# Starting the tiles of split weights at multiples of 128 bytes in a partition

## The chip, the cores and the metric

The kernel runs on one core of a Trainium2 chip. The metric is the device time of one execution in microseconds (us). The core's engines are named as the profile names them: PE is TensorE's matmul row, PEld its loads of the stationary operand, DVE is VectorE, ACT is ScalarE, POOL is GpSimd, and SP is SyncE, which here only issues transfers (DMAs). SBUF is the on-chip memory: 128 partitions, in each of which a tile takes a run of bytes. The start of that run, counted in bytes from the start of the partition, is the tile's address, and it is the same in every partition.

## What is computed

One layer of a decoder trunk over 256 tokens with a model width of 2048, all in float32. Almost all the work is products of activations with weights that are read once each:

```python
h = rmsnorm(x, attn_norm[l])
proj = h @ w_in[l]
...
mem_kv = rmsnorm(mem, mem_norm[l]) @ w_mem_kv[l]
...
y_gla = (o_gla * jax.nn.silu(gr)) @ w_br_gla[l]
y_sb = stick_breaking_mixer(q_sb, k_sb, sv) @ w_br_sb[l]
y_mem = memory_mixer(q_m, m_k, m_v) @ w_br_mem[l]
g = jax.nn.sigmoid(gates.reshape(B, T, N_BRANCH, D))
merged = g[:, :, 0] * y_gla + g[:, :, 1] * y_sb + g[:, :, 2] * y_mem
x = x + merged @ w_o[l]
h2 = rmsnorm(x, ffn_norm[l])
gate, up = jnp.split(h2 @ w_gate_up[l], 2, axis=-1)
x = x + (jax.nn.silu(gate) * up) @ w_down[l]
```

The three mixers between these products (gated linear attention, stick-breaking attention, attention into 256 memory tokens) are small beside them.

## The kernel before

Every weight is float32, and a product is made from three matmuls in the type fp32r. `split` (L116 to L125) turns a tile of raw weights into a high part `wh` (ACT, a cast, L121) and a low part `wl` (DVE, the difference, L122). The activations stand split in the same way, for instance as `xTh` and `xTl`. A product is then high times high, high times low, low times high: three matmuls that follow each other and add into one PSUM tile. In each of them the activations are the stationary operand (128x128, loaded by LDWEIGHTS before each matmul), and `wh` or `wl` is the moving operand, which is streamed through.

Two routines do this. `gemm` (L152) loads raw weights in tiles `raw` of 1 MB and splits them in pieces of 128x1024, each of which serves twelve matmuls of 512 columns (L176 to L178). `sgemm` (L184), used for the gates, the output projection and most of the feed-forward network, forms one step of a Strassen-like scheme on part of the depth: four quarters `rq` of 128x768 come by DMA, DVE adds them (L252), and seven products of 256 columns (L223 to L225) stand between ordinary ones of 512 columns (L246 to L248).

The tiles `wh` and `wl` come from `parts` (L148), each in a ring of `ring_bufs` buffers under its own tag. `parts` takes them from whichever of three pools is current (`kit`): `wring` for the memory and attention part (4 buffers of each), `mrg` for the merge and the output projection, and `ffn` for the feed-forward network (6 buffers of each). A tile of 128x1024 fp32r takes 4096 bytes in a partition, and the slices that matmuls read begin at whole multiples of 1024 bytes in it. In each pool other tiles lie behind the rings: `rq` in `mrg` and `ffn`, the sections and attention tiles behind `wring`, and `fh`, `fl`, `sdh`, `sdl` (the split activations of the feed-forward network) in `ffn`.

The order on each engine is the order of the code. Matmuls wait for their two operands; a cast into `wh` waits until the matmuls that read that buffer a ring earlier are done; DVE's subtraction waits for the cast. DMAs of weights are issued by SP in order, into rings of three `raw` and five `rq`. Small jobs of the mixers (`background`, taken up by `step`) are put between groups of matmuls.

Of the kernel before, what the change touches and what calls it, by code (L numbers as in the profile page):

```python
# [10 lines left out]
F32R = mybir.dt.float32r  # L11
# [5 lines left out]
P = 128  # L17
# [58 lines left out]
def trunk(ctx: ExitStack, tc: tile.TileContext, a, out):  # L76
# [6 lines left out]
    IT = 2 * NB  # L83
# [63 lines left out]

    def parts():  # L148

        return [kit.tile([P, IT], F32R, tag=f"w{x}", name=f"w{x}", bufs=ring_bufs) for x in "hl"]  # L150

    def gemm(xs, w, c0, row0=0, first=(), load=nc.sync.dma_start):  # L152

        o = [acc() for _ in range(2)]
        nk = len(xs)
        sizes = list(first)
        sizes += [min(KG, nk - k) for k in range(sum(sizes), nk, KG)]  # L160
        k0 = 0
        for n in sizes:
            xp = [x() if callable(x) else x for x in xs[k0 : k0 + n]]
            raw = loads()
            r0 = row0 + k0
            load(raw[:, :n], w[c0 // NB, :, r0 : r0 + n])
            for g in range(0, n, 2):
                m = min(2, n - g)
                wh, wl = (x[:].rearrange("p (k n) -> p k n", k=2) for x in parts())
                split(wh[:, :m], wl[:, :m], raw[:, g : g + m])  # L170
                for t in range(2):
                    s = slice(t * P, (t + 1) * P)
                    for j in range(m):
                        xh, xl = xp[g + j]
                        k = k0 + g + j
                        pe.matmul(o[t][:], xh[:, s], wh[:, j], start=k == 0, stop=False)  # L176
                        pe.matmul(o[t][:], xh[:, s], wl[:, j], start=False, stop=False)  # L177
                        pe.matmul(o[t][:], xl[:, s], wh[:, j], start=False, stop=k == nk - 1)  # L178
                step()
            k0 += n  # L180
        return o

    def sgemm(xs, forms, w, blk, row0=0, late=False):
# [22 lines left out]
        def form(src):  # L206
            hi, lo = (x[:, : SP * HB] for x in parts())
            split(hi, lo, src[:])
            return hi, lo
# [20 lines left out]
        def rest(k0, last=False):  # L230

            if k0 not in loaded:
                n = min(KG, nk - k0)
                raw = loads()
                c = ob + (k0 - 2 * SP) * NB
                nc.sync.dma_start(raw[:, :n], wb[:, c : c + n * NB].rearrange("p (k n) -> p k n", n=NB))
                for g in range(0, n, 2):
                    loaded[k0 + g] = raw[:, g : g + 2]
            wh, wl = (x[:].rearrange("p (k n) -> p k n", k=2) for x in parts())
            split(wh, wl, loaded[k0])  # L240
            for t in range(2):
                s = slice(t * P, (t + 1) * P)
                for j in range(2):
                    xh, xl = xs[k0 + j]
                    f, e = k0 + j == 2 * SP, last and j == 1
                    pe.matmul(o[t][:], xh[:, s], wh[:, j], start=f, stop=False, skip_group_check=True)  # L246
                    pe.matmul(o[t][:], xh[:, s], wl[:, j], start=False, stop=False, skip_group_check=True)  # L247
                    pe.matmul(o[t][:], xl[:, s], wh[:, j], start=False, stop=e, skip_group_check=True)  # L248
            step()
# [187 lines left out]
    kit = wring = tc.alloc_tile_pool(name="wring", bufs=1)  # L437
    ring_bufs = 4
# [406 lines left out]
    kit = mrg = tc.alloc_tile_pool(name="mrg", bufs=1)  # L845
    ring_bufs = 6
# [27 lines left out]
    hl = xpool.tile([P, KD, T], F32R, name="hl", tag="xTl")  # L874
# [25 lines left out]
    kit = ctx.enter_context(tc.tile_pool(name="ffn", bufs=1))  # L900
# [4 lines left out]
    for part in (range(0, 4), range(4, 8), range(8, NF)):  # L905
        fs, tiles = [], []
        for j in part:
# [6 lines left out]
            f = [kit.tile([P, 4, T], F32R, name=f"f{x}", bufs=4) for x in "hl"]  # L914
# [78 lines left out]
```

## Time and profile before

| | us |
|---|---|
| median of 3 runs | 1693.62 (1692.26 to 1694.8) |
| the profiled execution | 1692.7 |
| its span, first to last instruction | 1690.9 |
| PEld busy in the span | 1427.2 (84%) |
| DVE busy | 1286.2 (76%) |
| ACT busy | 930.7 (55%) |

The profiled execution is 0.92 us below the median, and 1.8 us of it lie outside its span. In the rows of the profile, "wh<-raw 128x1024" is an instruction that writes `wh` and reads `raw`; "acc<-wh,hl" is a matmul into the PSUM tile `acc` with `wh` as the moving operand and `hl` as the stationary one. The duration of a matmul includes its way through the array, so that matmuls overlap each other; what one costs is read from the distance between two starts. The column PEclk is the granted share of TensorE's clock.

### The profile page before, as it was taken

Reading aid. Unit: us, or ns where it says so; the run is one execution under the profiler, and the core shown is the slowest. Engines: PE = TensorE matmul, PEld = TensorE weight load, DVE = VectorE, ACT = ScalarE, POOL = GpSimd, SP = SyncE. Lnnn points to the kernel's source line nnn. Section 1 sums busy time; section 2 is a strip of 40 time slices with the busy share of each in tenths; the row PEclk is TensorE's granted clock in tenths of the full one; section 3 lists DMA queues with packets and bytes.
Section 4 is the critical chain, followed back from the end, with each engine's and each line's share of the span. In section 5 each row is a group of like instructions: output and inputs, shape, how many; then the busy total and the mean of one; then the engine's idle time right before and its main releaser. Section 6 shows DMA issues by size and latency. Waiting matters only on the chain.

```text
span 1690.9 us, 22452 instructions
## 1 busy us (share of the span) xinstructions
PE 1673.7 (99%) x8730; PEld 1427.2 (84%) x8730; DVE 1286.2 (76%) x1585; ACT 930.7 (55%) x1231; POOL 1.3 (0%) x6
## 2 busy tenths in 40 slices
PE   8999999999999999999999999999999999999999
PEld 6888888888877888888888788888888888888887
DVE  6756566664665578877889899988889988888863
ACT  6654454664653455555556566665555565555642
POOL 0000000000000000000000000000000000000000
PEclk9999999999999999999999999999999999999999
DMA  8765445445534556564566364655564555565562
GB/s 326 265 235 188 149 152 191 156 151 198 173 129 146 199 211 213 185 233 165 184 213 202 123 225 137 236 199 199 199 200 162 196 193 186 198 206 192 178 224 100
DMA packets 68682, 322.05 MB, mean 190 GB/s; under 512 B 7504, under 2 KB 12112, under 8 KB 41440
## 3 DMA queue, kind: packets, MB, share of 16 engines
q1 hardware_dynamic: 68112, 320.17, 55.4%
q8 instruction: 68, 1.11, 0.3%
q10 hardware_dynamic: 464, 0.45, 0.1%
q14 instruction: 38, 0.31, 0.0%
HBM read 318.50 MB, written 2.10 MB: 190 GB/s over the span
## 4 chain that ended last, share of the span: by engine, by line
PE 96%; DVE 1%; DMA 1%; ACT 0%; issue 0%; SPq 0%; DVEq 0%; ACTq 0%
PE acc L176 13%; PE acc L177 13%; PE acc L178 13%; PE acc L247 11%; PE acc L248 11%; PE acc L246 11%; PE tmp L225 4%; PE tmp L224 3%; PE tmp L223 3%; PE acc L225 3%; PE acc L223 3%; PE acc L224 3%; PE tmp L336 2%; DVE wl L122 1%; DMA raw<-in_w_mem_kv 0%; PE tmp L565 0%
## 5 line engine op out<-in xcount | busy, mean ns | idle before, releaser
L122 DVE TENSOR_TENSOR wl<-raw,wh 128x1024 fp32r<-128x1024 f32 (+1 forms) x459 | 558.7, 1220 | 271.7 <-ACT wh L121 268.1
L121 ACT CAST wh<-raw 128x1024 fp32r<-128x1024 f32 (+1 forms) x459 | 480.0, 1048 | 426.6 <-PE acc L178 265.8
L121 ACT CAST wh<-rq 128x768 fp32r<-128x768 f32 x294 | 244.8, 837 | 206.5 <-PE acc L248 80.0
L122 DVE TENSOR_TENSOR wl<-rq,wh 128x768 fp32r<-128x768 f32 x294 | 278.9, 954 | 27.1 <-ACT wh L121 23.5
L176 PE MATMUL acc<-wh,xTh 128*128 128x512 f32 x576 | 230.3, 400 | 0.0
L178 PE MATMUL acc<-wh,xTl 128*128 128x512 f32 x576 | 225.0, 391 | 0.0
L177 PE MATMUL acc<-wl,xTh 128*128 128x512 f32 x576 | 224.6, 390 | 0.0
L246 PE MATMUL acc<-wh,hh 128*128 128x512 f32 x440 | 174.4, 398 | 4.2 <-ACT wh L121 4.2
L247 PE MATMUL acc<-wl,hh 128*128 128x512 f32 x440 | 174.5, 396 | 1.1 <-DVE wl L122 0.9
L248 PE MATMUL acc<-wh,hl 128*128 128x512 f32 x440 | 173.0, 393 | 0.0
L252 DVE TENSOR_TENSOR rq<-rq 128x768 f32<-128x768 f32 x168 | 160.7, 957 | 4.4
L176 PE MATMUL acc<-wh,oh 128*128 128x512 f32 x320 | 125.3, 393 | 2.9 <-ACT wh L121 2.0
L178 PEld LDWEIGHTS acc<-wh,xTl 128*128 128x128 f32 x576 | 108.1, 188 | 23.3 <-issue 0.3
L176 PEld LDWEIGHTS acc<-wh,xTh 128*128 128x128 f32 x576 | 108.3, 188 | 22.1 <-issue 1.4
L177 PEld LDWEIGHTS acc<-wl,xTh 128*128 128x128 f32 x576 | 108.4, 188 | 21.7 <-issue 0.7
L177 PE MATMUL acc<-wl,oh 128*128 128x512 f32 x320 | 125.5, 392 | 0.5 <-DVE wl L122 0.5
L178 PE MATMUL acc<-wh,ol 128*128 128x512 f32 x320 | 125.3, 392 | 0.0
L246 PEld LDWEIGHTS acc<-wh,hh 128*128 128x128 f32 x440 | 83.5, 190 | 20.0 <-ACT wh L121 4.9
L248 PEld LDWEIGHTS acc<-wh,hl 128*128 128x128 f32 x440 | 83.8, 190 | 18.1
L247 PEld LDWEIGHTS acc<-wl,hh 128*128 128x128 f32 x440 | 84.0, 191 | 16.6 <-DVE wl L122 2.2
L176 PEld LDWEIGHTS acc<-wh,oh 128*128 128x128 f32 x320 | 60.1, 188 | 17.8 <-ACT wh L121 2.5
L177 PEld LDWEIGHTS acc<-wl,oh 128*128 128x128 f32 x320 | 60.5, 189 | 13.8 <-DVE wl L122 1.1
(319 smaller groups left out, 2999.3 us busy)
## 6 DMA issues: line engine op xcount, KB each, us to landing
raw<-in_w_in SPq DMA_DIRECT2D x72, 1024.0 KB, 4.8
raw<-in_w_gate_up SPq DMA_DIRECT2D x44, 1024.0 KB, 4.9
rq<-in_w_gate_up SPq DMA_DIRECT2D x88, 384.0 KB, 4.9
raw<-in_w_down SPq DMA_DIRECT2D x28, 1024.0 KB, 4.8
raw<-in_w_gate SPq DMA_DIRECT2D x16, 1024.0 KB, 6.9
raw<-in_w_mem_kv SPq DMA_DIRECT2D x15, 1024.0 KB, 4.9
rq<-in_w_gate SPq DMA_DIRECT2D x32, 384.0 KB, 5.2
rq<-in_w_down SPq DMA_DIRECT2D x32, 384.0 KB, 4.7
```

The costliest lines, as they stand in the source:

```text
L121: act.copy(hi, src)
L122: dve.tensor_tensor(lo, src, hi.bitcast(F32), op=ALU.subtract)
L176: pe.matmul(o[t][:], xh[:, s], wh[:, j], start=k == 0, stop=False)
L177: pe.matmul(o[t][:], xh[:, s], wl[:, j], start=False, stop=False)
L178: pe.matmul(o[t][:], xl[:, s], wh[:, j], start=False, stop=k == nk - 1)
L223: pe.matmul(dst, xh, hi[:, c], start=start and i == 0, stop=False, skip_group_check=True)
L224: pe.matmul(dst, xh, lo[:, c], start=False, stop=False, skip_group_check=True)
L225: pe.matmul(dst, xl, hi[:, c], start=False, stop=stop and i == SP - 1, skip_group_check=True)
L246: pe.matmul(o[t][:], xh[:, s], wh[:, j], start=f, stop=False, skip_group_check=True)
L247: pe.matmul(o[t][:], xh[:, s], wl[:, j], start=False, stop=False, skip_group_check=True)
L248: pe.matmul(o[t][:], xl[:, s], wh[:, j], start=False, stop=e, skip_group_check=True)
L252: dve.tensor_tensor(dst[:], a[:], b[:], op=ALU.add)
```

## The change

Each tile from `parts` is asked for with a start at a multiple of 128 bytes. No argument, before, means a multiple of 32.

```diff
     def parts():
 
-        return [kit.tile([P, IT], F32R, tag=f"w{x}", name=f"w{x}", bufs=ring_bufs) for x in "hl"]
+        return [kit.tile([P, IT], F32R, tag=f"w{x}", name=f"w{x}", bufs=ring_bufs, align_bytes=128) for x in "hl"]
```

No instruction is added, removed or moved on any engine. What changes is where tiles lie. These are the addresses in the two built programs, with the remainder by 128:

| tile (pool) | before | after |
|---|---|---|
| first `wh` (`wring`) | 137824 (96) | 137856 (0) |
| first `wl` (`wring`) | 154208 (96) | 154368 (0) |
| first `wh` (`mrg`) | 119392 (96) | 119424 (0) |
| first `wl` (`mrg`) | 143968 (96) | 144128 (0) |
| first `wh` (`ffn`) | 160352 (96) | 160384 (0) |
| first `wl` (`ffn`) | 184928 (96) | 185088 (0) |
| first `rq` (`mrg`) | 168544 (96) | 168736 (32) |
| first `fh` (`ffn`) | 183904 (96) | 184096 (32) |
| `sdh` (`ffn`) | 216672 (96) | 216864 (32) |
| `raw`, all three | 20608 (0) | 20608 (0) |
| `xTh` and `hh` | 64096 (96) | 64096 (96) |

All `wh` move up by 32 bytes and all `wl` by 160; what lies behind them in a pool moves up by 192. The tiles ahead of them stay, among them the raw weights and the stationary operands `xTh`, `xTl`, `hh`, `hl`, `oh`, `ol`, and the forms `sx` and `sf`.

## The prediction

> **What bounds the kernel now.** I read the page first, then the waits, then the matmuls in order of time. The page's first, second and fourth parts:
>
> ```profile
> span 1690.9 us, 22452 instructions
> PE 1673.7 (99%) x8730; PEld 1427.2 (84%) x8730; DVE 1286.2 (76%) x1585; ACT 930.7 (55%) x1231; POOL 1.3 (0%) x6
> PE 96%; DVE 1%; DMA 1%; ACT 0%; issue 0%; SPq 0%; DVEq 0%; ACTq 0%
> ```
>
> The chain that ended last is 96% matmuls. The longest waits by engine say the same from the other side:
>
> ```profile
> ACT wh L121 <- PE acc L178: 298.4, 186, 6.5
> DVE wl L122 <- ACT wh L121: 294.6, 252, 3.4
> ACT wh L121 <- PE acc L248: 202.0, 127, 2.5
> ```
>
> ACT waits about 500 us for matmuls to free a weight buffer, and DVE waits for ACT: the makers of weights are held up by PE, not PE by them. So an edit is worth what it does to the distance between matmul starts. In a quiet stretch of `gemm` (start, duration, engine and line):
>
> ```profile
> 599.84 0.39 PE L177 MATMUL acc<-wl,oh 128*128 128x512 f32 x1
> 600.06 0.39 PE L178 MATMUL acc<-wh,ol 128*128 128x512 f32 x1
> ...
> 605.96 0.39 PE L177 MATMUL acc<-wl,oh 128*128 128x512 f32 x1
> ```
>
> From the first to the last are 27 starts, 6.12 us, so 226.7 ns for 512 columns. There are 992 matmuls of L176 and 840 of L246 (count and busy time of one line over the whole span, PE then PEld), and each is one of three lines:
>
> ```profile
> 0.00:1691.00 1691.00, 393.16 (x992) 186.46 (x992) 1.00 0.56 190
> 0.00:1691.00 1691.00, 331.71 (x840) 158.79 (x840) 1.00 0.56 190
> 0.00:1691.00 1691.00, 250.64 (x882) 168.48 (x882) 1.00 0.56 190
> ```
>
> That is (992 + 840) x 3 = 5496 long matmuls, 5496 x 226.7 ns = 1246 us or 74% of the span. The last row is L223: 882 x 3 = 2646 short ones of 256 columns. Everything below hangs on what a long one pays.
>
> **What a long matmul pays.** After a pause in which the weights came late, the clock was granted at half for 6.6 us; first the windows row (PE, PEld, DVE, ACT, POOL, then PEclk), then matmuls in it:
>
> ```profile
> 963.90:970.50 6.60, 6.50 (x14) 4.63 (x15) 6.60 (x16) 4.00 (x6) 0.00 (x0) 0.50 0.92 339
> 966.66 0.63 PE L247 MATMUL acc<-wl,hh 128*128 128x512 f32 x1
> ...
> 970.07 0.60 PE L247 MATMUL acc<-wl,hh 128*128 128x512 f32 x1
> ```
>
> Eight starts in 3.41 us are 426 ns each. With each column a cycle of the array, full clock would make that 213.1 ns. The long matmul takes 226.7 at full clock, so it loses 13.6 ns there, and none at half clock. A fixed number of array cycles, such as a swap of stationary operands, would show at both. It is rather something that cannot feed the array at full speed: 2048 bytes in each partition in 226.7 ns. The loss is one part in 16 of the stream, and 128 bytes are one part in 16 of 2048. This is why the start of the tile may matter, and why I do not write the change off. The short ones:
>
> ```profile
> 1102.03 0.28 PE L223 MATMUL tmp<-wh,hh 128*128 128x256 f32 x1
> 1102.14 0.28 PE L224 MATMUL tmp<-wl,hh 128*128 128x256 f32 x1
> ...
> 1103.10 0.60 PE L336 MATMUL tmp<-cst,cv 128*128 128x128 f32 x4
> ```
>
> The first takes about 0.11 us, the next eight 0.96 / 8 = 120 ns. Half of a long one would be 113. Loads of the stationary operand, where the matmuls have two columns only, follow each other so:
>
> ```profile
> 439.09 0.19 PEld L703 LDWEIGHTS tmp<-cr,rd 128*128 128x128 f32 x1
> ...
> 439.76 0.19 PEld L703 LDWEIGHTS tmp<-cr,rd 128*128 128x128 f32 x1
> ```
>
> Six in 0.67 us, 112 ns each. So a short matmul is paced by its load of the stationary operand rather than by its stream, and a faster stream brings it at most 120 - 112 = 8 ns.
>
> **The change part by part.** No instruction is added or moved, so there is no new wait and no new order; three things can change.
>
> *ACT and DVE on other addresses.* The trace has sources at both kinds of start: `raw` at a multiple of 128, `rq` at 96 above one (duration as min/median/max):
>
> ```profile
> L121 ACT CAST wh<-raw x459: 604/1050/1116, 4.3 to 1670.7; 128x1024 fp32r<-128x1024 f32 x152, 128x512 fp32r<-128x512 f32 x1
> L121 ACT CAST wh<-rq x294: 817/838/902, 617.3 to 1608.3; 128x768 fp32r<-128x768 f32 x147
> L121 ACT CAST sxh<-raw x2: 1477/1482/1488, 611.1 to 855.9; 128x1536 fp32r<-128x1536 f32 x2
> L122 DVE TENSOR_TENSOR wl<-raw,wh x459: 691/1225/1229, 5.1 to 1671.8; 128x1024 fp32r<-128x1024 f32 x152, 128x512 fp32r<-128x512 f32 x1
> L122 DVE TENSOR_TENSOR wl<-rq,wh x294: 947/953/961, 618.6 to 1609.1; 128x768 fp32r<-128x768 f32 x147
> L122 DVE TENSOR_TENSOR sxl<-raw,sxh x2: 1753/1756/1758, 612.7 to 857.5; 128x1536 fp32r<-128x1536 f32 x2
> ```
>
> From `raw` alone ACT takes (1482 - 1050) / 512 = 0.84 ns an element, which gives 834 ns for 768 elements; from `rq` it takes 838. DVE takes (1756 - 1225) / 512 = 1.04 ns, which gives 959; from `rq` it takes 953. So a start of 96 instead of 0 is worth -6 to +4 ns in an instruction of about 900, as far as a read goes. A write at another start is not in the trace; I give it the same bounds. 753 casts x 4 ns are 3 us of ACT, hidden under its 500 us of waiting for PE. Taken at 0. The cover is thinnest in the feed-forward part:
>
> ```profile
> 900.00:1200.00 300.00, 295.65 (x1707) 260.15 (x1707) 269.79 (x325) 178.05 (x247) 0.00 (x0) 0.99 0.56 192
> ```
>
> DVE is busy for 270 of 300 us there. Six ns more on each of its 325 instructions are 2 us, still under the 30 that it has.
>
> *Transfers into `rq` at another start* (96 before, 32 after):
>
> ```profile
> rq<-in_w_gate_up SPq DMA_DIRECT2D x88, 384.0 KB, 4.9
> raw<-in_w_gate_up SPq DMA_DIRECT2D x44, 1024.0 KB, 4.9
> ```
>
> Both kinds land in 4.9 us though one is 2.7 times as large: the start is not what sets it. DMAs are busy for 0.56 of that stretch. Taken at 0; without their cover a wait would show at the casts.
>
> *The matmul's stream.* No tile in the trace of before that a matmul streams through starts at any other remainder than 96, so the price is not in the trace. Bounds for one long matmul: below, the whole loss goes, -13.6 ns; above, the worst distance that occurs with all operands there. After each pause comes a train like this:
>
> ```profile
> 1105.29 0.39 PE L247 MATMUL acc<-wl,hh 128*128 128x512 f32 x1
> ...
> 1106.45 0.39 PE L246 MATMUL acc<-wh,hh 128*128 128x512 f32 x1
> 1106.67 0.39 PE L247 MATMUL acc<-wl,hh 128*128 128x512 f32 x1
> ```
>
> Five starts in 1.16 us, 232 ns each, before it settles at 0.22 to 0.23. So +5.3 ns is the other end. Times 5496 these ends are -75 and +29 us. I take 0, the value of the nearest rows: the loss is there in every stage alike, with ACT, DVE and DMA busy or not; it goes with the length of the stream, as the 0.11 of the first short matmul suggests; and a cost of a bad start would come once in a matmul and not in proportion to its length. [...]
>
> Sum: 0 + 0 + 0. The profiled execution of 1692.7 stays; on the median's scale (0.9 higher) that is 1693.6.
>
> **The rivals.**
>
> *The start costs the whole loss.* If the stream is fetched in pieces of 128 bytes counted from its start, each piece that starts at 96 lies across two lines of 128, and each pays one step; from 0 none does. For it: the loss is just one part in 16, which is 128 bytes' share. Against it: nothing in the trace has another start. Long matmuls fall to 213.1: 5496 x 13.6 = 75 us, 1693.6 - 75 = 1619. If short ones gain their 8 ns too, 2646 x 8 = 21 more. DVE would not stop it: 5496 in 1691 us are 975 in 300 us, 13 us saved, and 287 is still above DVE's 270.
>
> *One line fewer.* If each cross of a line of 128 costs a sixteenth of the loss, 13.6 / 16 = 0.85 ns, a stream of 2048 bytes crosses 16 such lines from 96 and 15 from 0. 5496 x 0.85 = 4.7 us: 1689.
>
> *The stream falls in with the weight loads.* The train of 232 shows that the distance depends on how the stream and the load of the next stationary operand stand to each other: same operands, same engine, another phase. Now both start at 96; after the change the stream is 32 bytes apart from the load. If that makes the phase of the train the lasting one, each long matmul costs 5.3 ns more: 1693.6 + 29 = 1723, slower. It decides as soon as the matmuls in a quiet stretch stand over 0.6 ns further apart, for 0.6 x 5496 = 3.3 us is 0.2%, about what a measurement of this kernel can tell from no change. Against it: four kinds of stationary tiles all settle at 226.7. [...]
>
> **How the numbers follow.** No change: 0.50, as all rows are met by a limit that has nothing to do with the start. The whole loss or most of it goes: 0.22, since one part in 16 fits it too well to be left out. One line fewer: 0.10. Slower by the weight loads: 0.18. So faster is 0.32, the same 0.50, slower 0.18. The predicted time is that of the likeliest, 1693.6. The range takes in the first three cases, which hold 0.82: from 1618 to 1698. The likeliest alone would be 1690 to 1697.
>
> **What would show it.** In a quiet stretch the distance of long matmuls: 226.7 for my forecast, 213 to 214 for the first rival, 225.8 for the second, 232 for the third. Short ones at 120 in all cases but the first. The casts at 838 and 1050 and the subtractions at 953 and 1225 stay within 6 ns. I am wrong if the distance moves by over 0.6 ns, or if it stays and the time does not: then the waits of ACT and DVE must show a pause that was not there.

## The result and the profile after

| | before | after |
|---|---|---|
| median, us | 1693.24 | 1717.18 (1716.49 to 1717.35, 4 runs) |
| ratio | | 1.0138 [1.0126, 1.015] |
| span of the profiled execution, us | 1690.9 | 1715.4 |

The change makes the kernel 1.4% slower. This is the third rival's result, and it lies outside the range of the prediction. One correction to the table of addresses above: in its rows for `wh`, `wl` and `rq` the labels `mrg` and `ffn` are exchanged. All their remainders are the same, so nothing of the argument hangs on it.

The page of the kernel after, its first, second and fourth parts:

```profile
span 1715.4 us, 22452 instructions
PE 1698.2 (99%) x8730; PEld 1424.8 (83%) x8730; DVE 1288.1 (75%) x1585; ACT 930.1 (54%) x1231; POOL 1.3 (0%) x6
PE 96%; DVE 2%; DMA 1%; ACT 0%; issue 0%; SPq 0%; DVEq 0%; ACTq 0%
```

PE alone has grown, by as much as the span (24.5 us). The number of instructions and the share of matmuls in the chain that ended last are what they were; DVE and ACT are busy as long as before to within 2 us. The longest waits by engine:

```profile
ACT wh L121 <- PE acc L178: 313.2, 188, 6.6
DVE wl L122 <- ACT wh L121: 312.7, 264, 3.4
ACT wh L121 <- PE acc L248: 206.0, 125, 2.0
```

ACT waits 19 us longer for PE than before, and DVE 18 us longer for ACT: the makers of weights have more time, not less. The casts and subtractions (min/median/max in ns) and the transfers (KB, median us to landing) are as they were, to within 2 ns in each median and 0.3 us in the landing:

```profile
L121 ACT CAST wh<-raw x459: 602/1050/1087, 4.2 to 1694.7; 128x1024 fp32r<-128x1024 f32 x152, 128x512 fp32r<-128x512 f32 x1
L121 ACT CAST wh<-rq x294: 817/836/863, 628.6 to 1630.9; 128x768 fp32r<-128x768 f32 x147
L122 DVE TENSOR_TENSOR wl<-raw,wh x459: 692/1224/1228, 5.0 to 1695.8; 128x1024 fp32r<-128x1024 f32 x152, 128x512 fp32r<-128x512 f32 x1
L122 DVE TENSOR_TENSOR wl<-rq,wh x294: 945/951/961, 629.9 to 1631.8; 128x768 fp32r<-128x768 f32 x147
rq<-in_w_gate_up SPq DMA_DIRECT2D x88, 384.0 KB, 4.6
raw<-in_w_gate_up SPq DMA_DIRECT2D x44, 1024.0 KB, 4.9
```

What is left is the matmul. A quiet stretch of `gemm` in order of time (start, duration, engine, line):

```profile
580.47 0.39 PE L177 MATMUL acc<-wl,oh 128*128 128x512 f32 x1
...
589.72 0.39 PE L178 MATMUL acc<-wh,xTl 128*128 128x512 f32 x1
```

From the first to the last are 40 starts in 9.25 us: 231.3 ns, where the kernel before has 226.7. The starts between these rows are 0.23, 0.23 and 0.24 us apart in turn and repeat with the three matmuls of a product. This is the quicker of two cycles that the kernel falls into: in the memory and attention part the three take 693 ns together in about a third of the products and 700 in more than half. Over all pairs of consecutive long matmuls (5254, as many as before) the sum of the distances goes from 1216.7 to 1242.6 us, +25.9; for those under 260 ns, which leaves out pauses, the mean goes from 227.9 to 232.7 ns. The sum for the short ones goes from 295.7 to 294.0, -1.7. Together that is about the growth of the span. It is spread over all stages: the kernel after is 11.1 us behind by 600 us, 17.5 by 990 and 24.5 at the last matmul.

### The profile page after: what moved, and what is told of

Same layout as the page of the kernel before. It is cut to its first block, busy times and chain, and to the rows that moved or that the text cites. A ratio compares the mean times of both kernels' runs of the same rounds, so it can differ in the third digit from the quotient of the medians.

```text
span 1715.4 us, 22452 instructions
## 1 busy us (share of the span) xinstructions
PE 1698.2 (99%) x8730; PEld 1424.8 (83%) x8730; DVE 1288.1 (75%) x1585; ACT 930.1 (54%) x1231; POOL 1.3 (0%) x6
## 4 chain that ended last, share of the span: by engine, by line
PE 96%; DVE 2%; DMA 1%; ACT 0%; issue 0%; SPq 0%; DVEq 0%; ACTq 0%
PE acc L178 14%; PE acc L177 13%; PE acc L176 13%; PE acc L248 11%; PE acc L247 11%; PE acc L246 11%; PE tmp L225 3%; PE tmp L224 3%; PE tmp L223 3%; PE acc L225 3%; PE acc L224 3%; PE acc L223 2%; PE tmp L336 2%; DVE wl L122 1%; DMA raw<-in_w_mem_kv 0%; PE tmp L537 0%
## 5 line engine op out<-in xcount | busy, mean ns | idle before, releaser
L176 PE MATMUL acc<-wh,xTh 128*128 128x512 f32 x576 | 232.5, 404 | 0.0
L178 PE MATMUL acc<-wh,xTl 128*128 128x512 f32 x576 | 227.9, 396 | 0.0
L176 PE MATMUL acc<-wh,oh 128*128 128x512 f32 x320 | 126.7, 397 | 3.0 <-ACT wh L121 2.3
L178 PEld LDWEIGHTS acc<-wh,xTl 128*128 128x128 f32 x576 | 108.1, 188 | 25.4 <-issue 0.3
L176 PEld LDWEIGHTS acc<-wh,xTh 128*128 128x128 f32 x576 | 107.9, 187 | 24.8 <-ACT wh L121 0.8
L178 PE MATMUL acc<-wh,ol 128*128 128x512 f32 x320 | 127.5, 398 | 0.0
L176 PEld LDWEIGHTS acc<-wh,oh 128*128 128x128 f32 x320 | 59.9, 188 | 19.9 <-ACT wh L121 2.7
```

## The experiments

Three theories stood at the outset. **A**: what counts is the distance between the start of the stream and the start of the stationary operand (0 before; after, 32 for `wh` and 160 for `wl`, and with `fh` and `fl`, which move up by 192 themselves, 160 and 32 the other way). **B**: a stream from a multiple of 128 is slow by itself. **C**: what counts is the distance between `wh` and `wl`, which the change makes 128 bytes larger. All edits are made to the kernel before, and all ratios are against it on the same chip.

### Everything up by 32 bytes

```diff
+    main.tile([P, 8], F32, tag="shift", name="shift", bufs=1)
```

This small tile stands ahead of all tiles but the raw weights and the constants, so `wh`, `wl` and the stationary operands all start at a multiple of 128.

> All large tiles, the stationary operands too, move up by 32 bytes, so that the weights start at a multiple of 128 as after the change, but stream and stationary operand start at the same remainder as before. Theory A (what counts is how the start of the stream stands to the start of the stationary operand that is loaded meanwhile): long matmuls at 226.7 ns, 1693 us. Theory B (a stream that starts at a multiple of 128 is slow by itself): 231 to 233 ns, 1717 us. Theory C (what counts is the distance from wh to wl, which the change made 128 bytes larger): it is as before here, so 226.7 ns, 1693 us.

Measured 1693.96 against 1694.06 us, ratio 0.9995 [0.9986, 1.0005]. Its matmuls in order of time:

```profile
568.90 0.39 PE L177 MATMUL acc<-wh,oh 128*128 128x512 f32 x1
...
578.20 0.39 PE L179 MATMUL acc<-wh,xTl 128*128 128x512 f32 x1
```

Those are 41 starts in 9.30 us, 226.8 ns each, with a stream from a multiple of 128. B falls: the new start costs nothing if the stationary operand has it too.

### Both streams up by 32, at their old distance from each other

```diff
+    PADS = {'wring': (32, 0), 'mrg': (32, 0), 'ffn': (32, 0)}
...
+            n = PADS[kit.name][i]
+            if n and (kit.name, x) not in padded:
+                padded.add((kit.name, x))
+                kit.tile([P, n // 4], F32, tag=f"pad{x}", name=f"pad{x}", bufs=1)
```

Two numbers for each pool: the bytes put ahead of `wh` and between `wh` and `wl`. What lies behind the rings moves along, so in the last stage `fh` and `fl` move with the streams. (Lines that an edit puts in raise the line numbers in the rows: L186 to L188 here are L176 to L178 before.)

> wh and wl both move up by 32 bytes, their distance stays as before; the stationary operands stay, apart from the split activations fh and fl of the feed-forward network, which lie behind the weights and move with them. Theory A: long matmuls at 230 to 235 ns, 1705 to 1730 us; only the last stage (L176 to L178 with fh and fl, the last 70 us) keeps 226.7 ns, because there both moved. Theory B: 1717 us, the last stage as slow as the others. Theory C: 226.7 ns everywhere, 1693 us.

Measured 1711.57 us, ratio 1.0101 [1.0086, 1.0116]. First the attention stage, then the last stage of the same execution:

```profile
580.83 0.39 PE L187 MATMUL acc<-wl,oh 128*128 128x512 f32 x1
...
590.16 0.39 PE L188 MATMUL acc<-wh,xTl 128*128 128x512 f32 x1
...
1675.63 0.39 PE L188 MATMUL acc<-wh,fl 128*128 128x512 f32 x1
...
1684.70 0.39 PE L186 MATMUL acc<-wh,fh 128*128 128x512 f32 x1
```

There are 40 starts in each piece: 9.33 us or 233.3 ns in the first, 9.07 us or 226.8 ns in the second. The streams start at the same remainder in both pieces; only the stationary operand has moved along in the second. C falls as the cause, for the distance of `wh` and `wl` is the old one, and A is shown with a control inside one run.

### Only `wl` moved, and other distances

Only the numbers of `PADS` change. With (0, 128) in all pools `wh` stays and `wl` goes up by 128:

> Only wl moves, by 128 bytes; wh stays. Theory A with a period of 128 bytes: 226.7 ns, 1693 us; with a longer period, matmuls of wl alone change. Theory B: the remainder by 128 is as before, 1693 us. Theory C: the distance is as after the change, 231 to 233 ns, 1717 us.

Measured 1704.67 us, ratio 1.0062 [1.0047, 1.0077]. In the memory and attention part the next start comes 231.3 ns after one of `wh`, whose distance is still 0, and 231.8 ns after one of `wl`. These means mix several cycles. In 102 of the 626 products seen whole there only `wl` is slow, as in these rows, where the starts are 0.22, 0.24 and 0.22 us apart:

```profile
574.92 0.39 PE L186 MATMUL acc<-wh,oh 128*128 128x512 f32 x1
575.14 0.40 PE L187 MATMUL acc<-wl,oh 128*128 128x512 f32 x1
575.38 0.39 PE L188 MATMUL acc<-wh,ol 128*128 128x512 f32 x1
575.60 0.39 PE L186 MATMUL acc<-wh,oh 128*128 128x512 f32 x1
```

In others all three are slow, with 236, 234 and 230 ns or 232, 232 and 234. That only matmuls of `wl` change thus holds for a part of the products. The distances of the two starts don't fix the cycle by themselves, and a matmul that is in step with its own operands can be slow beside one that isn't. Whether the distance of `wh` and `wl`, which this edit changes too, has a part in that is not shown.

Four kernels then moved both streams by amounts that differ from pool to pool:

```diff
+    PADS = {'wring': (64, 0), 'mrg': (96, 0), 'ffn': (128, 0)}
...
+    PADS = {'wring': (256, 0), 'mrg': (512, 0), 'ffn': (192, 0)}
...
+    PADS = {'wring': (384, 0), 'mrg': (160, 0), 'ffn': (320, 0)}
...
+    PADS = {'wring': (352, 0), 'mrg': (448, 0), 'ffn': (224, 0)}
```

> wh and wl move up together, by 64 bytes in the memory and attention part (the first 600 us), by 96 in the merge and output projection, by 128 in the feed-forward network. Theory A with a period of 128 bytes: 226.7 ns in the feed-forward network, other distances than 226.7 in the two parts before, to either side (213 to 240 ns). Theory B: remainders by 128 are 32, 64 and 96 and none is 0, so 226.7 ns throughout, 1693 us. Theory C: 1693 us.

> wh and wl move up together against the stationary operands: by 256 bytes in the memory and attention part, by 512 in the merge and output projection, by 192 in the feed-forward network. Theory A with a period of 256 bytes: 226.7 ns in the first two parts, about 231 in the third. With a period of 512: 226.7 in the second part alone. With no period up to 512: 226.7 nowhere but in the last stage, where fh and fl moved with the weights. If some distance is better than none, long matmuls below 226 ns show in that part.

> wh and wl move up together by 384 bytes in the memory and attention part, by 160 in the merge and output projection, by 320 in the feed-forward network. Theory A: 228 to 235 ns in all three unless the period is 128, 160 or less, 226.7 in the last stage; below 226 ns in a part where the distance is better than none. About 1705 to 1715 us.

> wh and wl move up together by 352 bytes in the memory and attention part, by 448 in the merge and output projection, by 224 in the feed-forward network. Theory A: 228 to 235 ns in all three, 226.7 in the last stage; below 226 ns in a part where the distance is better than none. About 1705 to 1715 us.

In this order they took 1707.11 us, ratio 1.007 [1.0053, 1.0087]; 1693.31, 1.0 [0.9989, 1.0012]; 1705.02, 1.0062 [1.004, 1.0085]; 1711.23, 1.0103 [1.0074, 1.0132]. The mean distance of two starts in ns, by the distance of the stream's start above that of the stationary operand (long: pairs under 260 ns, so with the trains after pauses, and over whatever cycles occur; the short ones, under 150 ns, only in `mrg` and `ffn`):

| distance, bytes | long | short |
|---|---|---|
| 0 | 227.5 to 228.6 | 119.5 |
| 32 | 233.2 | 116.8 |
| 64, and 320 | 229.3, 229.2 | 116.1 |
| 96, and 352 | 233.3, 233.4 | 119.9 |
| 128, and 384 | 232.8, 232.8 | 118.4 |
| 160 | 234.0 | 117.8 |
| 192, and 448 | 232.9, 233.1 | 114.7, 114.2 |
| 224 | 233.4 | 118.3 |
| 256 and 512 | 227.5, 227.9 | |

The pattern has a period of 256 bytes: 256 and 512 give what 0 gives, and 320, 352, 384 and 448 give what 64, 96, 128 and 192 give. The expectation of a period of 128 bytes is missed: at 128 the long matmuls take 232.8 ns. In the kernel with 256, 512 and 192, first long matmuls at a distance of 256, then short ones at 192:

```profile
569.50 0.39 PE L187 MATMUL acc<-wl,oh 128*128 128x512 f32 x1
...
578.57 0.39 PE L188 MATMUL acc<-wh,xTl 128*128 128x512 f32 x1
...
1026.03 0.28 PE L235 MATMUL tmp<-wh,sfl 128*128 128x256 f32 x1
...
1027.73 0.28 PE L235 MATMUL acc<-wh,hl 128*128 128x256 f32 x1
```

The 40 long starts take 9.07 us, 226.8 ns each. The 15 short ones take 1.70 us, 113 ns each, where the kernel before takes 120. Of the distances tried, 0 suits long matmuls best and 192 short ones; that kernel comes out even because in `ffn` the one pays for the other.

### Which stationary operand: in use, or being loaded

```diff
-    xtiles = [xpool.tile([P, KD, T], F32R, name=f"xT{x}", tag=f"xT{x}") for x in "hl"]
+    xtiles = []
+    for x in "hl":
+        xtiles.append(xpool.tile([P, KD, T], F32R, name=f"xT{x}", tag=f"xT{x}"))
+        if x == "h":
+            xpool.tile([P, 8], F32, tag="shift", name="shift")
```

All tiles behind `xTh` go up by 32, so only products with `xTh` (and `hh`, in its place) have a distance. While a matmul runs, the stationary operand of the next one is loaded (in the kernel before, the load for the matmul that starts at 600.06 starts at 599.84, together with the matmul ahead of it); if only the one in use or only the one being loaded counted, one of the three matmuls would keep its 227.

> All large tiles move up by 32 bytes, as in the run all32, but for xTh (and hh, which takes its place). So the high part of these activations starts 32 bytes below weights and low part, and everything else starts alike. Theory A: where oh, fh, sx or sf are stationary, 226.7 ns; where xTh and xTl or hh and hl are, about two in three long matmuls are slower, 228 to 235. If it is the operand loaded meanwhile that counts, the matmul of wl (during which the low part is loaded) is the one that keeps about 227, and both matmuls of wh are slow. If it is the operand in use, the matmul with the low part keeps 227, and both with the high part are slow. Theory B: about 1717 us, all slow. About 1703 us by theory A.

Measured 1706.85 us, ratio 1.0077 [1.0048, 1.0106]:

```profile
240.09 0.40 PE L176 MATMUL acc<-wh,xTh 128*128 128x512 f32 x1
...
245.45 0.39 PE L178 MATMUL acc<-wh,xTl 128*128 128x512 f32 x1
```

These are 23 starts in 5.36 us, 233 ns, and all three lines are slow (`wh,xTh` 235 to 236, `wl,xTh` 233, `wh,xTl` 231 to 232), while quiet stretches with `oh` and `fh` keep 226.7. The buffers of `wh` and `wl` that are streamed against `xTh` and against `oh` are the same, filled by ACT and DVE in the same way, so it isn't these engines' accesses that make the difference. Neither operand alone decides. The excess over 226.7 is largest (9 ns) where both operands stand apart, 6 ns where only the one in use does, and 5 ns where only the one being loaded does; that each adds a part fits this, but wasn't tested by itself, and as a matmul in step can be slow beside one out of step (the run in which only `wl` moved), the question stays open.

### What the loss is made of

The loss meant here is the prediction's estimate: 226.7 ns measured at full clock, less half of the 426 ns measured at a granted clock of 0.50, so 13.6 ns. That a long matmul can run at 213.1 ns no run shows. If the stationary operand's load takes reading time from the stream, another load should change the loss. Three kernels changed the load. The first reads every second token, with its 128 columns 8 bytes apart instead of 4 (it mixes up the order of the tokens), at distances of 128, 0 and 64 in the three pools:

```diff
-                    s = slice(t * P, (t + 1) * P)
+                    s = slice(t, t + 2 * P - 1, 2)
```

> The long matmuls read their stationary operand with a step of two tokens (one tile the even tokens, the other the odd ones, instead of the first and the second half), so the order of tokens in the output is another and the mixers work on mixed tokens; the work is the same in amount. The load of 128 columns then covers 1024 bytes instead of 512. The streams start 128 bytes above the stationary operand in the memory and attention part, at the same remainder in the merge and output projection, 64 bytes above in the feed-forward network. Theory A says that load and stream meet where they read the same lines by 256 bytes at the same time: with a load that moves on at another pace the loss of 13.6 ns itself changes, to either side, and with it the three parts differ from 226.7 and from each other. If the loss of 13.6 ns is the stream's own, long matmuls stay at 226.7 or above in all parts, none below 226.

Measured 1713.07 us, ratio 1.0108 [1.009, 1.0127]; long matmuls are 231.4, 232.8 and 233.2 ns apart. In `mrg` the starts have the distance 0 (4 bytes less for the odd tokens) and it is slow all the same, at 232.3 and 233.4 ns: equal starts didn't help a load that reads every second element. All parts lie above 226.7, so the run doesn't tell whether the loss of 13.6 ns is the load's or the stream's own. That load and stream read the same lines at the same time, as the expectation takes theory A, is not shown.

The other two load fewer columns in `gemm`, and so leave out part of the products: 64, or 16 (`P // 8` in place of `P // 2`, here with `mrg` up by 32 bytes as well).

```diff
-                        pe.matmul(o[t][:], xh[:, s], wh[:, j], start=k == 0, stop=False)
...
+                        m_ = P if k in (0, nk - 1) else P // 2
+                        s = slice(t * P, t * P + m_)
+                        pe.matmul(o[t][:m_], xh[:, s], wh[:, j], start=k == 0, stop=False)
```

> In the routine of ordinary products (L176 to L178) every matmul but those of the first and the last depth step takes 64 columns of its stationary operand instead of 128, so half of each token tile gets only two of its depth steps; the stream of 512 columns and its address stay. The load of the next operand is half as long. If the load takes the 13.6 ns from the stream: about half of it is left, 220 ns in the quiet stretches of this routine. If the stream pays it by itself: 226.7 ns as before. At 220 ns some 2500 matmuls save 6.7 ns each, 17 us.

> As half, but 16 columns of the stationary operand instead of 64 (a load of 64 bytes in a partition), and in the merge and output projection wh and wl lie 32 bytes further up. If the load reads against the stream, long matmuls of the ordinary routine fall by an eighth of the loss, to 215 to 217 ns, and in the merge part too, whatever the distance. If the stream pays by itself, 226 to 230 ns with so short a load as well; if it pays at its start by how it stands to the load's start, the merge part still differs from the memory and attention part.

They took 1699.38 us, ratio 1.0037 [1.0021, 1.0053], and 1703.27 us, 1.0061 [1.0038, 1.0084]. Loads and long matmuls with 64 columns:

```profile
574.31 0.13 PEld L180 LDWEIGHTS acc<-wh,ol 128*64 128x64 f32 x1
...
231.54 0.40 PE L178 MATMUL acc<-wh,xTh 128*64 128x512 f32 x1
...
237.99 0.39 PE L179 MATMUL acc<-wl,xTh 128*64 128x512 f32 x1
```

and with 16:

```profile
574.13 0.09 PEld L188 LDWEIGHTS acc<-wh,oh 128*16 128x16 f32 x1
...
231.32 0.40 PE L188 MATMUL acc<-wh,xTh 128*16 128x512 f32 x1
...
239.88 0.40 PE L189 MATMUL acc<-wl,xTh 128*16 128x512 f32 x1
```

The loads shrink from 0.19 to 0.13 and 0.09 us. The matmuls stand 6.45 / 28 = 230.4 and 8.56 / 37 = 231.4 ns apart: more than with full loads, though the distance is 0, and neither of the expected values (220 or 226.7 with 64 columns). A loss in proportion to the load's columns would have shrunk to a half and an eighth. With 16 columns a distance of 32 costs nothing more (230.3 ns in `mrg`, 231.1 at distance 0 in `wring`), where full loads go from 226.7 to 233: there the short load is the faster one. This fits the reading that 226.7 is a favourable cadence into which full loads from the same remainder fall, and not an undisturbed pace to which a bad start adds a cost. It isn't shown: the matmul itself also works on fewer columns here, and that wasn't tested apart from the load.

### The short matmuls alone

In the table long matmuls are best at distance 0 (227.5 to 228.6 ns) and short ones at 192 (114.7 and 114.2), and both can be had: the short ones read the first 768 of the 1024 elements of a tile, so their quarters can lie 192 bytes (48 elements) further up in it, while the long ones stay.

```diff
-            hi, lo = (x[:, : SP * HB] for x in parts())
+            hi, lo = (x[:, 48 : 48 + SP * HB] for x in parts())
```

> The kernel before, except that the split quarters (the streams of the short matmuls) lie 192 bytes further on inside their tile of 4096 bytes; long matmuls as before. Theory A, with what the runs sweep_b and sweep_d showed at a distance of 192 bytes (short ones at 113 to 114 ns instead of 120): 2646 x 6.6 ns = 17 us less, 1676 us, long ones unchanged at 226.7. If the gain of the short ones in those runs came from something else that was moved there (rq or cv), 120 ns and 1694 us.

Measured **1685.4** against 1694.25 us, ratio **0.9944 [0.993, 0.9957]**: faster than both kernels. The page, then the short matmuls of a product and what follows them:

```profile
span 1683.1 us, 22452 instructions
...
647.82 0.28 PE L224 MATMUL tmp<-wl,xTh 128*128 128x256 f32 x1
...
649.82 0.39 PE L246 MATMUL acc<-wh,xTh 128*128 128x512 f32 x1
650.05 0.39 PE L247 MATMUL acc<-wl,xTh 128*128 128x512 f32 x1
650.27 0.39 PE L248 MATMUL acc<-wh,xTl 128*128 128x512 f32 x1
650.50 0.39 PE L246 MATMUL acc<-wh,xTh 128*128 128x512 f32 x1
```

From the first row to the first long matmul are 17 starts in 2.00 us, 117.6 ns, which is also the mean; 113 came only in 17 products whose first two starts are about 0.2 us apart. The expected size is therefore missed: 2646 x 1.9 ns (119.5 less 117.6) are 5 us. Another gain was not foreseen: the long matmuls behind the short ones begin at 0.23 at once, without the train of 232, and their mean falls from 228.4 to 226.9 ns in `ffn` and from 227.9 to 226.9 in `mrg`, about 4 us together. Two more places for the quarters, the first 64 bytes up, the second 176 in `mrg` and 208 in `ffn`:

```diff
+            hi, lo = (x[:, 16 : 16 + SP * HB] for x in parts())
...
+            off = 44 if kit.name == "mrg" else 52
+            hi, lo = (x[:, off : off + SP * HB] for x in parts())
```

> As short192, but the split quarters lie 64 bytes further on inside their tile. In the run sweep_c short matmuls at this distance took 116 ns after long ones at 229. If the distance alone sets them, 116 ns here too, 2646 x 4 = 11 us less than before, 1683 us; if it is how the long matmul ahead stands in time, anything from 113 to 120, and long ones at 226.7.

> As short192, but with 176 bytes in the merge and output projection and 208 in the feed-forward network. If 192 is one point of a broad stretch, short matmuls at 113 to 115 ns in both parts; if the banks that matter are 16 or 32 bytes wide, one of the two or both at 116 to 120.

They took 1690.29 us, ratio 0.9983 [0.9972, 0.9994], and 1690.17, 0.9977 [0.9966, 0.9989], with short means of 118.0, and of 118.8 and 119.0 ns. So most of the gain is gone 16 bytes to either side of 192. That banks of 16 or 32 bytes are behind this, as the expectation supposes, no run shows. In the table short matmuls took 116.1 ns at 320 bytes, which is 64 by the period of 256, and 114.7 at 192, both times beside long ones that were out of step. So for short matmuls the distance alone doesn't set the pace; that what ran just ahead of them does too fits these runs and the products at 113, but wasn't tested by itself.

## Why the prediction was wrong

- *PE is the bound, the makers wait for it*: right. ACT's longest wait, for L178, grew from 298.4 to 313.2 us.
- *Casts and subtractions at other addresses, 0*: right. 838 became 836 ns, 1050 stayed.
- *Transfers into `rq`, 0*: right. 4.9 became 4.6 us.
- *Short matmuls, 120 ns in all cases but the first rival*: nearly. Their mean went from 119.5 to 118.7 ns, worth 1.7 us. The reason given, the pace of their loads (112 ns), was not shown: their own pace, 113 to 120 ns over the runs, moves with the distance and, as it seems, with what ran ahead of them.
- *The matmul's stream, "I take 0, the value of the nearest rows"*: **this step failed.** It measured +4.9 ns on each of the 5254 distances between long matmuls (25.9 us), inside the bounds of -13.6 and +5.3 that the step had set up itself. The reasons for the 0 took the start of the stream by itself, with a bad start paid once in a matmul; that was the author's estimate, and no run shows it. The runs showed in its place a relation of two starts. Alone, the start is free (everything up by 32: 226.8 ns); against the stationary operand, 32 bytes cost 6 ns. Why the distance of the two starts counts is not shown.
- *"Four kinds of stationary tiles all settle at 226.7"* was held against the third rival. It was no evidence: all four, and both streams, started at a remainder of 96 by 512 bytes, so the trace held one value of what the change was about to vary. The only row in which anything about the pair varied was the train of 232, and it pointed the right way.
- *The third rival*, 1723 us at 232 ns, named the relation that counts and nearly its size: 1717.2 us and 231 to 233 ns. Its price was 0.4 ns a matmul too high, it reckoned with 32 bytes for both streams where `wl` stands 160 away, and its chance of 0.18 was too low. That the lasting cadence is the same thing as the train wasn't shown.
- *The first two rivals* fall: no long matmul settled at 213 or 225.8 ns in any of the runs, at any of eight remainders. That the loss at full clock is one part in 16 led to nothing that a run bore out. The 213.1 ns was an estimate from 426 ns at half the clock; that each column takes a cycle of the array, and that the stream is read in lines of 128 bytes, was assumed, and no run shows it.

Open: why the pace has a period of 256 bytes, and why a long matmul in step takes 226.7 ns at full clock where half of the 426 ns at half clock would be 213.1. With shorter loads it took 230.4 and 231.4 ns, so the loads' reading isn't shown to be the cause. Open too is what chooses among the cycles. With loads of adjacent columns, distances of long matmuls that aren't multiples of 32 bytes weren't tried.

## What to carry to other kernels

For fp32r matmuls of 512 columns back to back, start the moving and the stationary tiles at the same remainder by 256 bytes (here means of 227.5 to 228.6 ns a start at the distances 0, 256 and 512, and of 229.2 to 234.0 at the others tried): an alignment asked for one of them can move it against the other (here `wh` by 32 bytes and `wl` by 160, for 1.4% of the time), and a tile put in ahead can do the same unnoticed (here both streams by 32, for 1.0%). The check is the distance of starts in a quiet stretch, for a matmul's own duration (0.39 us before and after) doesn't show it. And where all rows of a trace share one value of the thing that a change will vary, their agreement says nothing on the change; the row in which it varies, however odd, weighs more.

## What was not expected of the hardware

- The pace of matmuls depends on the distance between the starts of their two operands, with a period of 256 bytes: 226.7 ns for 512 columns in step, cycles with means of 229 to 234 ns otherwise.
- With starts in step, shorter loads of the stationary operand go with a slower stream: 226.7 ns with 128 columns, 230.4 with 64, 231.4 with 16. At a distance of 32 bytes it is the other way: 233 with 128, 230.3 with 16.
- The same tiles at the same distances settle into different cycles in one execution: with `wl` alone 128 bytes up, products of three take 684 to 690 ns or 698 to 700.
- Matmuls of 256 columns did best elsewhere, at 192 bytes: down to 113 ns, where the kernel before has a mean of 119.5. Shifting them alone inside their tiles gained 0.56%, partly in the long matmuls behind them.
